# Rotating 96 images by 180 degrees: the first 2 KB of each row of the first load go through ACT's DMA queue

## The chip, the cores and the metric

The kernel runs on one core of a Trainium2 chip. The metric is device time in microseconds (us) of one execution. Before the change the median of three runs is 121.97 us (121.9 to 122.13).

## What is computed

```python
x = np.random.randn(32, 3, 256, 256).astype(np.float32)
out = np.rot90(x, k=2, axes=(-2, -1))
```

Each of the 96 images (256 x 256 float32, 256 KB) is turned by 180 degrees. Seen as one row of 65,536 numbers, an image is simply reversed. 25.17 MB are read and 25.17 MB are written; there is no arithmetic.

## The kernel before

An image is cut into four segments of E = 16,384 numbers (64 KB). A segment becomes a row of one SBUF partition, so 128 segments make a tile of 8.39 MB and three tiles hold everything: `A` and `Bt` hold the even and the odd segments of the first 64 images, `Ct` all segments of the last 32. Reversing an image means two things: the order of its four segments is reversed, which the stores do by their addresses (`::-1` in L53 to L54), and each segment is reversed within its row, which VectorE does in place.

Each tile is loaded by one DMA of 128 rows of 64 KB. Two DMA queues are in use. SyncE (SP) issues the loads of `A` (L64) and then `Ct` (L67), and after them every store; in the profile its queue is q1. ScalarE (ACT) issues only the load of `Bt` (L66); its queue is q10. Both queues feed the same 16 DMA engines, and each engine has 8 of the 128 rows of a tile. Within a queue the rows go in the order of their issue. Ahead of the load of `Bt` stands a VectorE memset of `Bt[:, 0:256]` (L65). The load overwrites what it wrote, so ACT has to wait for the memset before it issues.

`swap(t, lo, w)` (L56) exchanges the `w` numbers from `lo` on with their mirror image at the other end of the row, in three VectorE copies (L47): the far end reversed into the scratch tile `T`, the near end reversed into the far end, and `T` into the near end. `turn(t, lo, hi)` (L69) runs swaps of up to J = 2,048 numbers until `lo` reaches `hi`; half a row (8,192) makes a whole turn. The copies are kept in the order of the program (L47), which is written out by hand:

```python
turn(A, 0, half - J)        # L76: three of A's four swaps
store(A, 0, 0, LEAD)        # L77: 1 KB of each row, wants only the first swap
turn(Bt, 0, MID)            # L78: waits for the load of Bt
turn(A, half - J, half)     # L79: A's last swap
store(A, 0, LEAD, E)        # L80: the other 63 KB of each row
turn(Bt, MID, half)         # L81
store(Bt, 1, 0, E)          # L82
turn(Ct, 0, half)           # L83
store(Ct, 2, 0, E)          # L84
```

So the large store of `A` (L80) stands behind the first two swaps of `Bt` (L78) in VectorE's order, and all stores stand behind the load of `Ct` in SP's queue.

Of the kernel before, what the change touches and what calls it, by code (L numbers as in the profile page):

```python
# [2 lines left out]

os.environ.setdefault("NEURON_RT_ULTRASERVER_MODE", "4")

# [4 lines left out]


@with_exitstack
def kernel(
    ctx: ExitStack,
    tc: tile.TileContext,
    x: bass.AP,
    out: bass.AP,
):
    nc = tc.nc  # L20
    P = 128

    B, C, H, W = x.shape
    L = H * W
    G = 32
    E = L // 4
    J = E // 8

    xr = x.rearrange("b c h w -> (b c) (h w)").rearrange(
        "m (s e) -> (m s) e", s=4)  # L30
    om = out.rearrange("b c h w -> (b c) (h w)").rearrange(
        "m (s e) -> m s e", s=4)
    rows = 2 * P
    x4 = [xr[0:rows:2], xr[1:rows:2], xr[rows:rows + P]]
    o4 = [om[0:2 * G, 1::2], om[0:2 * G, 0::2], om[2 * G:3 * G]]

    pool = ctx.enter_context(tc.tile_pool(name="slots", bufs=1))
    A = pool.tile([P, E], x.dtype, tag="A")
    Bt = pool.tile([P, E], x.dtype, tag="B")
    Ct = pool.tile([P, E], x.dtype, tag="C")  # L40
    T = pool.tile([P, J], x.dtype, tag="T")

    def back(t, lo, hi):
        return t[:, hi - 1:(lo - 1 if lo else None):-1]

    def copy(dst, src):
        tc.keep_in_program_order(nc.vector.tensor_copy(out=dst, in_=src))  # L47

    def load(t, g, lo, hi, queue=nc.sync):
        return queue.dma_start(out=t[:, lo:hi], in_=x4[g][:, lo:hi])  # L50

    def store(t, g, lo, hi):
        return nc.sync.dma_start(  # L53
            out=o4[g][:, ::-1, lo:hi], in_=t[:, lo:hi])  # L54

    def swap(t, lo, w):  # L56
        hi = E - lo - w
        copy(T[:, 0:w], back(t, hi, hi + w))
        copy(t[:, hi:hi + w], back(t, lo, lo + w))
        copy(t[:, lo:lo + w], T[:, 0:w])  # L60

    MID = 2560
    LEAD = 256
    load(A, 0, 0, E)  # L64
    nc.vector.memset(Bt[:, 0:256], 0.0)  # L65
    load(Bt, 1, 0, E, nc.scalar)  # L66
    load(Ct, 2, 0, E)  # L67

    def turn(t, lo, hi):  # L69
        while lo < hi:  # L70
            w = min(J, hi - lo)
            swap(t, lo, w)
            lo += w

    half = E // 2
    turn(A, 0, half - J)  # L76
    store(A, 0, 0, LEAD)  # L77
    turn(Bt, 0, MID)  # L78
    turn(A, half - J, half)  # L79
    store(A, 0, LEAD, E)  # L80
# [6 lines that stand above are left out]
# [1 line left out]
_INS = ['x']  # L88
_OUTS = [((32, 3, 256, 256), 'float32')]


# [23 lines left out]
```

## Time and profile before

| what | value |
|---|---|
| device time, median of 3 runs | 121.97 us (121.9 to 122.13) |
| device time of the profiled execution | 121.9 us |
| its span | 120.1 us |
| VectorE busy | 44.9 us, 40 instructions |
| one 128x2048 copy | 1.23 us |
| DMA traffic | 50.33 MB, 1008 packets, mean 419 GB/s |
| load of `A`, from issue to landing | 38.7 us |
| load of `Bt` | 43.1 us |
| load of `Ct` | 60.1 us |

The span is what the profile shows from the first instruction to the last, and 1.8 us of the device time lie around it. In the profile's DMA lines a packet is one row of a transfer on one engine, or the 4-byte write with which an engine tells that its share of a transfer has landed; each transfer has 128 rows and 16 such writes, and seven transfers give 1008 packets. A DMA view of a stretch counts the packets that start in it, by queue. "SPq" and "ACTq" are the instructions with which SP and ACT issue transfers.

### The profile page before, as it was taken

To read this page: it belongs to the slowest core of one execution; us is meant where nothing else is said; L and a number is where in the kernel's file an instruction comes from. 1 tells how busy PE (TensorE), PEld (TensorE's weight loads), DVE (VectorE), ACT (ScalarE), POOL (GpSimd) and SP (SyncE) were. 2 spreads that over 40 slices of the span, in tenths; PEclk is the share of its full clock that TensorE was granted. 3 is DMA by queue.
4 is the path that set the end of the run, shared out by engine and by line. 5 is a ranking of instruction groups with operands and counts; after the bars stand their busy time and mean duration, and the time that the engine had idled before them with its cause. 6 is when DMAs were issued, how large, how long until landed. Compare 5 with 4: busy or idle time off the path is not lost.

```text
span 120.1 us, 97 instructions
## 1 busy us (share of the span) xinstructions
DVE 44.9 (37%) x40; POOL 0.2 (0%) x4
## 2 busy tenths in 40 slices
DVE  0000000000000899999999999999400000000000
POOL 0000000000000000000000000000000000000000
DMA  9888988898889988998899777988898889888980
GB/s 349 349 349 371 677 349 349 349 698 349 349 349 633 415 349 349 546 502 349 349 387 687 344 344 344 687 349 349 349 698 349 349 349 698 349 349 349 677 371 0
DMA packets 1008, 50.33 MB, mean 419 GB/s; under 512 B 112, under 2 KB 240, under 8 KB 240
## 3 DMA queue, kind: packets, MB, share of 16 engines
q1 hardware_dynamic: 864, 41.94, 81.3%
q10 hardware_dynamic: 144, 8.39, 16.1%
HBM read 25.17 MB, written 25.17 MB: 419 GB/s over the span
## 4 chain that ended last, share of the span: by engine, by line
DVE 38%; DMA 32%; issue 1%
DMA A<-in_x_dram 32%; DVE T L47 13%; DVE Bt L47 9%; DVE A L47 8%; DVE Ct L47 8%
## 5 line engine op out<-in xcount | busy, mean ns | idle before, releaser
L47 DVE COPY T<-A 128x2048 f32<-128x2048 f32 x4 | 4.9, 1226 | 38.4 <-DMA A<-in_x_dram 38.3
L47 DVE COPY T<-Bt 128x2048 f32<-128x2048 f32 (+2 forms) x5 | 5.1, 1014 | 0.2
L47 DVE COPY Bt<-T 128x2048 f32<-128x2048 f32 (+2 forms) x5 | 5.1, 1014 | 0.2
L47 DVE COPY Bt<-Bt 128x2048 f32<-128x2048 f32 (+2 forms) x5 | 5.1, 1013 | 0.2
L47 DVE COPY T<-Ct 128x2048 f32<-128x2048 f32 x4 | 4.9, 1227 | 0.1
L47 DVE COPY Ct<-T 128x2048 f32<-128x2048 f32 x4 | 4.9, 1227 | 0.1
L47 DVE COPY A<-T 128x2048 f32<-128x2048 f32 x4 | 4.9, 1227 | 0.1
L47 DVE COPY A<-A 128x2048 f32<-128x2048 f32 x4 | 4.9, 1227 | 0.1
L47 DVE COPY Ct<-Ct 128x2048 f32<-128x2048 f32 x4 | 4.9, 1226 | 0.1
L65 DVE MEMSET Bt<- 128x256 f32 x1 | 0.3, 272 | 0.9 <-PEq L99 0.9
L99 POOL MEMSET const-bfloat16-1.0<- 128x1 bf16 x1 | 0.1, 102 | 0.0
L99 POOL MEMSET const-uint8-127<- 128x1 uint8 x1 | 0.1, 102 | 0.0
L99 POOL MEMSET const-float32-0.0<- 128x1 f32 x1 | 0.1, 99 | 0.2 <-issue 0.2
L99 POOL MEMSET const-float32-1.0<- 128x1 f32 x1 | 0.1, 99 | 0.0
## 6 DMA issues: line engine op xcount, KB each, us to landing
out_dram<-A SPq DMA_DIRECT2D x1, 8064.0 KB, 20.9
out_dram<-A SPq DMA_DIRECT2D x1, 128.0 KB, 18.4
A<-in_x_dram SPq DMA_DIRECT2D x1, 38.7
Bt<-in_x_dram ACTq DMA_DIRECT2D x1, 43.1
Ct<-in_x_dram SPq DMA_DIRECT2D x1, 60.1
out_dram<-Bt SPq DMA_DIRECT2D x1, 29.6
out_dram<-Ct SPq DMA_DIRECT2D x1, 33.9
```

Source lines behind the costliest of these rows:

```text
L47: tc.keep_in_program_order(nc.vector.tensor_copy(out=dst, in_=src))
L65: nc.vector.memset(Bt[:, 0:256], 0.0)
L99: nc = _bacc.Bacc("TRN2", target_bir_lowering=False, num_devices=1)
```

## The change

The load of `A` is split by columns. SP loads columns 512 to 16,384 (62 KB of each row), and ACT loads columns 0 to 512 (2 KB of each row) ahead of its load of `Bt`. The memset is removed, so ACT's issues wait for nothing.

```diff
     MID = 2560
     LEAD = 256
-    load(A, 0, 0, E)
-    nc.vector.memset(Bt[:, 0:256], 0.0)
+    FIRST = 512
+    load(A, 0, FIRST, E)
+    load(A, 0, 0, FIRST, nc.scalar)
     load(Bt, 1, 0, E, nc.scalar)
     load(Ct, 2, 0, E)
```

In the program that is built, ACT issues two transfers in place of one, and neither waits for a semaphore. SP's order is as before. VectorE has one instruction less; its first copy (`T` from the far end of `A`) waits for the 62 KB transfer, and its second copy, which reads the near end of `A`, waits for the 2 KB transfer. The order of the copies and of the stores is the same. There are eight transfers in place of seven.

## The prediction

> **What bounds the kernel now.** I read the page first, then the DMA issues, then the DMA queues in short stretches of time, then the timeline of SP and VectorE.
>
> ```profile
> span 120.1 us, 97 instructions
> ...
> DMA  9888988898889988998899777988898889888980
> ...
> q1 hardware_dynamic: 864, 41.94, 81.3%
> q10 hardware_dynamic: 144, 8.39, 16.1%
> ```
>
> The two queues' packets fill 97.4% of the 16 DMA engines' time: the transfers are the bound, and there is no gap anywhere in the span. From q10, which carried only `Bt`, comes the price of a row: 16.1% of 120.1 us on 16 engines over 128 rows is 0.161 x 120.1 x 16 / 128 = **2.42 us for a 64 KB row** on its engine. An engine has 8 rows of each of 3 loads and 3 stores, 48 x 2.42 = 116 us. The page's chain of waits, which puts 38% on VectorE's copies, is misleading as a price list: those copies (44.9 us in all) lie beside transfers. They only matter where they keep the engines without a row to move.
>
> ```profile
> out_dram<-A SPq DMA_DIRECT2D x1, 8064.0 KB, 20.9
> out_dram<-A SPq DMA_DIRECT2D x1, 128.0 KB, 18.4
> A<-in_x_dram SPq DMA_DIRECT2D x1, 38.7
> Bt<-in_x_dram ACTq DMA_DIRECT2D x1, 43.1
> Ct<-in_x_dram SPq DMA_DIRECT2D x1, 60.1
> ```
>
> `A` and `Bt` land at nearly the same time (0.73 + 38.7 = 39.4 us, 1.16 + 43.1 = 44.3), `Ct` at 1.16 + 60.1 = 61.3. So the two queues share the engines while both have rows. How they share decides this case. Below are the DMA views of four stretches; each line is a queue with the packets that start in the stretch, their MB, and their share of it. First 4.5 to 5.5 us, then 7 to 7.8, then 9.5 to 10.2, then 38.4 to 40.6.
>
> ```profile
> q1 hardware_dynamic: 16, 1.05, 241.8%
> ```
>
> ```profile
> q10 hardware_dynamic: 16, 1.05, 302.4%
> ```
>
> ```profile
> q1 hardware_dynamic: 16, 1.05, 345.6%
> ```
>
> ```profile
> q10 hardware_dynamic: 16, 1.05, 109.9%
> q1 hardware_dynamic: 16, 0.00, 0.4%
> ```
>
> All 16 engines move one row of q1, then one of q10, then one of q1: the queues take turns, and **a turn is one row**. The last stretch shows more: q1's turn there is the 4-byte completion write of `A` (16 packets, 0.00 MB), and after these 4 bytes it is q10's turn again with the last row of `Bt`. A turn is counted in packets and not in bytes. The order on each engine is thus A A B A B A B A B A B A B A B, completion of `A`, B, C C C ...; the stretch from 1.5 to 3 us has one row of q1 on each engine, 4.5 to 5.5 the second, and q10 comes in third because ACT issues 0.43 us after SP.
>
> What feeds the engines when the loads are done? The rest of `A`, and only just:
>
> ```profile
> 59.76 0.55 SPq L53 DMA_DIRECT2D out_dram<-A  x1
> ```
>
> SP issues it at 59.76 us, when VectorE is done with `A`'s last swap, and the engines run out of loads and of the 128 KB lead store at 60.97 to 61.2 us, when the first 63 KB rows start. An issue takes about 1 us to become a first row (0.73 to 1.74 for `A`'s load), so there is next to no slack: whatever delays this issue leaves the engines empty.
>
> **The change part by part.** *Memset removed.* It costs 0.27 us on an idle VectorE, whose first copy starts at 39.47 us. Worth nothing itself. What it did is hold ACT's issue:
>
> ```profile
> 0.73 0.38 SPq L50 DMA_DIRECT2D A<-in_x_dram  x1
> 0.85 0.27 DVE L65 MEMSET Bt<- 128x256 f32 x1 [0.85 <-PEq L99]
> 1.16 0.38 ACTq L50 DMA_DIRECT2D Bt<-in_x_dram  x1
> 1.16 0.43 SPq L50 DMA_DIRECT2D Ct<-in_x_dram  x1
> ```
>
> Without it ACT issues the 2 KB rows at about 0.73, and `Bt` 0.43 later at 1.16, as now. SP's issue, with which the rows start at 1.74, is unmoved.
>
> *Rows.* The bytes are the same. SP's eight rows of an engine shrink from 64 to 62 KB, 8 x 2.42 x 2/64 = 0.60 us less. ACT's eight rows of 2 KB are not in the trace. The nearest are the lead store's 1 KB rows: eight of them and a completion write take the 0.65 us from 60.32 (first completion of `Ct`) to 60.97, 0.08 us each. At the large rows' rate 2 KB take 0.076; as the 1 KB row plus 1 KB more at that rate, 0.12. Eight cost 0.60 to 0.96 us, so the net is 0 to +0.36. Below nothing: the first row of `A` is followed by the second after 2.98 us (1.74 to 4.72), 0.57 more than a row, and small rows could fill that, so down to -0.57. I take +0.15, the middle of the first two ends. The added completion write (9 ns-sized in the 0.4% above) is nothing.
>
> *Turns.* This is the whole change. ACT's queue now begins with eight 2 KB rows. If each takes a turn, as the 4-byte write did, the order is A a A a ... (a is 2 KB), then C B C B ...: `A` no longer shares with `Bt`. `A` would land after 8 large rows in place of 15, 7 x 2.42 less the 0.15 = 16.8 us earlier, and VectorE would start at 39.47 - 16.8 = 22.7 us; its second copy up to one row later, if SP is a row ahead as now. `Bt` loses as much: it shares with `Ct` and comes last of the 24 large rows. Now the last of these is `Ct`'s, landing at 61.3; so `Bt` lands there, plus 0.15, plus 0.08 for a lead row that has its turn before `Bt`'s completion: 61.5 in place of 44.3.
>
> *What is behind that.* VectorE starts `A` at 22.7 and ends its three swaps near 34. Then it stands before `Bt`'s first swap (L78) until 61.5. Behind that wait in its order are `A`'s last swap and, through it, SP's issue of `A`'s 63 KB store; the only other thing in q1 is the lead store, 0.65 us of work. From `Bt`'s first copy to that issue the trace has 50.82 to 59.76 = 8.94 us (6 copies of 1.23, 3 of 0.43, 0.03 between them; hidden today under `Ct`'s rows). So the issue comes at 61.5 + 8.94 = 70.4. The first row follows an issue by 1.01 us for `A`'s load (0.73 to 1.74); an issue of a store takes 0.55 us where that took 0.38, so 1.0 to 1.2: first rows at 71.4 to 71.6, where they now are at 60.97. That is +10.5 to +10.7. An empty start may cost again what the first one did, 0 to 0.57: I take +0.3. Sum 10.6 + 0.3 = **+10.9 us**. Its ends: without the 0.15 and without a restart cost +10.3, with 0.36 for the small rows and the whole 0.57 +11.5; a start filled by small rows would take 0.57 off the low end, to +9.8.
>
> *Later.* `A`'s store then runs 8 x 2.38 = 19 us to about 91. `Bt`'s store is issued 10.55 us after `A`'s (70.31 - 59.76), at 81, `Ct`'s at 70.4 + 25.7 = 96.1 with `Bt`'s rows running to 110: no second gap. VectorE's early start on `A` buys nothing, as nothing of `A` but 128 KB may leave before L80.
>
> Against the profiled execution's 121.9 us (0.07 below the median of 121.97): 121.9 + 10.9 = **132.8 us**, bounds of this case 131.7 to 133.4.
>
> **The rivals.** *(1) The 2 KB rows go together (not slower).* If an engine takes ACT's small rows in one turn, or they are there before SP's first row and run ahead, only 0.6 to 0.96 us pass before `Bt` gets its turns against `A`. Then the order is A A a..a A B A B ...: `A` lands a row earlier and `Bt` a row later than now, 46.7, still before VectorE wants it at about 48.4 (37.05 + 11.35 of copies). The issue of `A`'s store stays ahead of 60.97. Time: 121.9 with -0.57 to +0.36, so 121.3 to 122.3. The point from which it decides is how many small rows pass without a large row of `A` between them: each brings `Bt` forward by 2.42 us, and from five of the eight on the gap of 10.9 is closed. For it: the trace has never had rows this small against another queue. Against it: the 4-byte write, smaller still, used up a turn, and no two rows of q10 ran together while q1 had any; SP's and ACT's issues come at the same time, and all 16 engines would have to do it, as VectorE waits for all.
> [...]
>
> *(2) A few small rows run ahead.* If one, two or three of the eight are through on every engine before SP's first row, `Bt` starts its turns so many rows earlier: 132.8 less 2.42 each, 130.4, 128.0 or 125.5 (four would leave 123.1). For it: without the memset ACT's issue is no longer later than SP's, and a small row takes a thirtieth of a large one. Against it: now SP had two rows in before q10's first, and SP issues no later.
>
> **How the numbers follow.** The forecast with its full gap has 0.76, rival 2 0.11 (0.08 of it for one or two rows), rival 1 0.13. The predicted time is the forecast's, 132.8. The range has to hold 8 in 10: the forecast's 131.7 to 133.4, 0.5 more above because the trace has no store that starts on empty engines (the 0.2 that I added for its issue could be some 0.7), and down to rival 2's two rows, less 0.2: 127.8 to 133.9. That holds the forecast but for its tails (0.72) and 0.08 of rival 2; rival 1 and three rows are left out. A measurement here tells about 0.2% (0.24 us) from no change. Rival 1's span of 121.3 to 122.3 splits into faster 0.03, same 0.08, slower 0.02; all else is slower: faster 0.03, same 0.08, slower 0.89.
>
> **What would show it.** Right: `A` lands near 22 to 25 us (the 2 KB part last), `Bt` near 61.5 together with `Ct`; VectorE's largest waits are two, some 22 us for `A` and some 26 for `Bt`; the issue of `A`'s 63 KB store is near 70.4; the DMA digits have about three slices near 0 from 61 to 71 us, and the queue's shares still sum to about 117 us of a span near 131; every later row is shifted by the gap. Wrong: `Bt` lands near 45 to 52, `A` near 37, and the digits stay full; or q10's first rows run together in the first 3 us. A gap of another length with `Bt` at 61.5 would mean that the price of the copies or of the restart is off.

## The result and the profile after

The changed kernel takes **132.75 us** (132.57 to 132.78, 5 runs) against 121.98 (121.9 to 122.34, 5 runs) beside it: ratio 1.0875, 95% interval 1.0864 to 1.0887. The profiled execution took 132.57 us with a span of 130.8, so the span grew by 10.7 us and what lies around it did not. The forecast was 132.8.

The page of the changed kernel: span, busy tenths of VectorE and DMA in 40 slices of 3.3 us, GB/s, and the two queues.

```profile
span 130.8 us, 99 instructions
...
DVE  0000001999300000002999999999930000000000
...
DMA  9799799797797797891007779779799797797790
GB/s 311 321 442 521 321 524 448 321 641 321 321 641 321 321 641 321 361 601 40 0 0 316 316 316 631 316 316 636 321 561 401 321 641 321 321 641 321 321 641 0
...
q1 hardware_dynamic: 864, 41.68, 74.3%
q10 hardware_dynamic: 288, 8.65, 15.3%
```

The hole is in the middle, at the 20th to the 22nd slice (62 to 72 us): engines that were never empty there now are. The queues together fill 89.6% of 130.8 us, 117.2 us, as before (97.4% of 120.1, 117.0). No work was added; time without work was. VectorE has a hole of its own just ahead of it.

The DMA issues of the changed kernel (engine, KB, us from issue to landing):

```profile
A<-in_x_dram SPq DMA_DIRECT2D x1, 7936.0 KB, 21.8
A<-in_x_dram ACTq DMA_DIRECT2D x1, 256.0 KB, 22.0
...
Bt<-in_x_dram ACTq DMA_DIRECT2D x1, 60.2
Ct<-in_x_dram SPq DMA_DIRECT2D x1, 60.0
```

`A` lands 17 us earlier than before (38.7) and `Bt` 17 us later (43.1), now together with `Ct`. The DMA view from 4.7 to 5.3 us (queue: packets started, MB, share) shows how:

```profile
q1 hardware_dynamic: 16, 1.02, 390.3%
q10 hardware_dynamic: 16, 0.03, 14.0%
```

Within this 0.6 us each engine starts one 2 KB row of q10 and one 62 KB row of q1. It goes on like that to the end of `A`: from 4 to 21.2 us each queue starts 112 rows, 7.11 MB and 0.23 MB. From 24 to 24.7 us `Bt` has its first row:

```profile
q10 hardware_dynamic: 16, 1.05, 345.4%
```

Before, that was at 7.14 us. What it costs is in the timeline of the changed kernel (start, us, instruction, idle time before it and what ended it), in SP's timeline from 66 to 72 us, and in the DMA views from 61.3 to 71 us and from 71 to 73:

```profile
22.53 1.23 DVE L47 COPY T<-A 128x2048 f32<-128x2048 f32 x1 [22.53 <-DMA A<-in_x_dram]
...
61.46 1.23 DVE L47 COPY T<-Bt 128x2048 f32<-128x2048 f32 x1 [27.62 <-DMA Bt<-in_x_dram]
...
66.63 1.23 DVE L47 COPY T<-A 128x2048 f32<-128x2048 f32 x1
...
70.41 1.23 DVE L47 COPY T<-Bt 128x2048 f32<-128x2048 f32 x1
```

```profile
70.40 0.54 SPq L53 DMA_DIRECT2D out_dram<-A  x1
```

```profile
DMA packets 0, 0.00 MB, mean 0 GB/s; under 512 B 0, under 2 KB 0, under 8 KB 0
```

```profile
q1 hardware_dynamic: 16, 1.03, 121.0%
```

VectorE waits 27.6 us for `Bt`, then does two swaps of `Bt`, then `A`'s last swap from 66.63 to 70.4. Only then can SP issue `A`'s 63 KB store, and from 61.3 to 71 us no row starts. The store's first rows start at 71.60 in place of 60.97, and each takes 1.21 x 2 = 2.42 us from the start.

### The profile page after: what moved, and what is told of

Same layout as the page of the kernel before. It is cut to its first block, busy times and chain, and to the rows that moved or that the text cites. A ratio compares the mean times of both kernels' runs of the same rounds, so it can differ in the third digit from the quotient of the medians.

```text
span 130.8 us, 99 instructions
## 1 busy us (share of the span) xinstructions
DVE 44.6 (34%) x39; POOL 0.2 (0%) x4
## 3 DMA queue, kind: packets, MB, share of 16 engines
q1 hardware_dynamic: 864, 41.68, 74.3%
q10 hardware_dynamic: 288, 8.65, 15.3%
## 4 chain that ended last, share of the span: by engine, by line
DVE 34%; another core or an unknown queue 21%; DMA 17%; issue 1%; DVEq 0%
DMA A<-in_x_dram 17%; DVE T L47 11%; DVE Bt L47 8%; DVE Ct L47 8%; DVE A L47 8%; DVEq L47 0%
## 5 line engine op out<-in xcount | busy, mean ns | idle before, releaser
L47 DVE COPY T<-Bt 128x2048 f32<-128x2048 f32 (+2 forms) x5 | 5.1, 1014 | 27.8 <-DMA Bt<-in_x_dram 27.6
L47 DVE COPY T<-A 128x2048 f32<-128x2048 f32 x4 | 4.9, 1227 | 22.6 <-DMA A<-in_x_dram 22.5
```

## Experiments

The theory: q1 and q10 take turns on every engine row by row whatever the rows' size, so eight small rows at the head of ACT's queue put `Bt` eight turns back (seven against before, where `A` was a row ahead already), and the loss is the gap before `A`'s store, which stands behind `Bt`'s first swaps. Times of before beside the experiments were 121.98 to 122.02 us.

### The memset alone removed

```diff
-    nc.vector.memset(Bt[:, 0:256], 0.0)
```

> Only the memset is removed; A is loaded whole by SP. Theory (queues take turns packet by packet, and what counts is which rows have their turns first): both issues come at 0.73 us, so the order is A B A B from the start, the second row of A is no longer ahead, A's completion write comes after Bt's eighth row, one turn of 2.42 us later than before. A lands near 41.9 us in place of 39.4, Bt too near 41.9 in place of 44.3; A's large store is issued at 62.2 in place of 59.76 and the engines are empty for about 2.3 us: 124.2 us (123.9 to 124.6). Rival (the loss of the change comes from the missing memset, not from the small rows): near 132.7. Rival (the memset is of no account): 121.9.

Measured **124.35 us** (124.26 to 124.64), ratio 1.0197 (1.0182 to 1.0212). The timeline of this kernel:

```profile
41.88 1.23 DVE L47 COPY T<-A 128x2048 f32<-128x2048 f32 x1 [41.88 <-DMA A<-in_x_dram]
```

and its DMA view from 4.5 to 5.5 us:

```profile
q10 hardware_dynamic: 16, 1.05, 241.9%
```

The second row of every engine is `Bt`'s, where it was `A`'s before. That one turn makes VectorE 2.41 us later (41.88 against 39.47) and the kernel 2.4 us slower. The memset was no dead weight: its 0.43 us of delay bought `A` a turn.

### The change with the memset put back

```diff
     load(A, 0, 0, FIRST, nc.scalar)
+    nc.vector.memset(Bt[:, 0:256], 0.0)
     load(Bt, 1, 0, E, nc.scalar)
```

> The changed kernel with the memset put back ahead of Bt's load. Theory: Bt's issue comes at 1.16 us with or without it, since ACT first issues the 2 KB rows, and all that decides is the eight small rows: 132.7 us (132.5 to 132.9), Bt landing near 61.4. Rival (the missing memset makes the loss): 121.9.

Measured **132.8 us** (132.62 to 132.83), ratio 1.0882 (1.0864 to 1.09). VectorE waits 27.6 us for `Bt`, as in the changed kernel. So the loss of the change is that of the small rows.

### The small rows on SP's queue

```diff
-    load(A, 0, FIRST, E)
-    load(A, 0, 0, FIRST, nc.scalar)
+    load(A, 0, 0, FIRST)
+    load(A, 0, FIRST, E)
     load(Bt, 1, 0, E, nc.scalar)
```

> The same split, but SP issues the 2 KB rows too, ahead of its 62 KB rows, and ACT issues only Bt, without a memset. Theory: now SP's queue spends eight turns on small rows while Bt moves a 64 KB row in each of its own, so the two change places: Bt lands near 22.5 us and A near 41.9, after 16 large rows. VectorE waits for A; its large store is issued near 62.2 and the gap is about 2.4 us: 124.3 us (123.9 to 124.8). Rival (the split into small rows costs in itself, whichever queue has them): near 132. Rival (SP's queue goes first whatever its rows are): A near 23 and 132 as well.

Measured **124.56 us** (124.48 to 124.85), ratio 1.0214 (1.0199 to 1.023). The issues of this kernel:

```profile
A<-in_x_dram SPq DMA_DIRECT2D x1, 7936.0 KB, 40.9
...
Bt<-in_x_dram ACTq DMA_DIRECT2D x1, 27.3
```

The two tiles have changed places, as a matter of which queue holds the small rows. The size for `Bt` was missed: 28 us in place of 22.5. From 1.5 to 3 us the trace has

```profile
q10 hardware_dynamic: 15, 0.98, 165.6%
q1 hardware_dynamic: 48, 0.10, 48.5%
```

Several engines had thus started two or more of SP's small rows before `Bt`'s first row, three on average; those rows went without a row of `Bt` between them, so that SP came to its large rows earlier and `Bt` shared its last turns with `A`. That is the mechanism of the prediction's second rival, seen here and not in the changed kernel.

### Unneeded rows in place of the split: eight, four, two

`A` is loaded whole again; ACT first loads 256 KB of the input into `T`, which nobody reads. The shape is 128 x 2 KB, 64 x 4 KB or 32 x 8 KB:

```diff
-    nc.vector.memset(Bt[:, 0:256], 0.0)
+    nc.scalar.dma_start(out=T[0:128, 0:512], in_=x4[2][0:128, 0:512])
```

> Before without the memset, A whole on SP, and ACT first loads 256 KB that nobody needs into T (128 rows of 2 KB, eight on each engine), then Bt. The extra 256 KB cost 0.6 us of the engines' time wherever they go. Theory: whose data the small rows carry is of no account, only that there are eight: as the changed kernel plus 0.6, A near 23, Bt near 62.0, A's large store issued near 71.0: 133.2 us (132.8 to 133.6). Rival (it is the split of A, its second copy's wait, or its shorter rows): near 122.5.

> As the kernel with eight unneeded rows, but the 256 KB are 64 rows of 4 KB, four on each engine. Theory (turns are counted in rows): Bt's completion comes after 21 large rows in place of 24, at about 54.8 us, A near 30; A's large store is issued near 63.7, the gap is about 3.3 us: 125.9 us (125.3 to 126.5). Rival (what counts is the bytes ahead of Bt): 133.2 as with eight rows.

> As above with 32 rows of 8 KB, two on each engine. Theory: Bt's completion after 19 large rows, near 49.9 us, A near 35; A's large store is issued near 58.9, ahead of the end of the loads: no gap, 122.5 us (122.3 to 122.8), before plus the 0.6 of the extra bytes. Rival (bytes): 133.2.

The load of `Bt` in the three kernels, in this order:

```profile
Bt<-in_x_dram ACTq DMA_DIRECT2D x1, 61.2
```

```profile
Bt<-in_x_dram ACTq DMA_DIRECT2D x1, 57.1
```

```profile
Bt<-in_x_dram ACTq DMA_DIRECT2D x1, 49.9
```

| rows on each engine | expected us | measured us |
|---|---|---|
| eight of 2 KB | 133.2 | 133.39 (133.34 to 133.51), ratio 1.0926 (1.0906 to 1.0945) |
| four of 4 KB | 125.9 | 127.08, 129.6, 129.81, 129.94 |
| two of 8 KB | 122.5 | 123.80 (123.74 to 123.8), ratio 1.014 (1.0125 to 1.0155) |

The same 256 KB cost 11.4, 5 to 8 and 1.8 us: it is the count of rows that counts, and neither the bytes, nor the split of `A`, nor its second copy's wait. The sizes of the two lower doses were missed, and the four runs with four rows fall apart into one of 127.08 and three near 129.8, so no ratio is given for them. In the profiled four-row run (129.6) `A` had two rows in before q10's first, as in before: from 4.5 to 6.5 us all 16 starts are q1's.

```profile
q1 hardware_dynamic: 16, 1.05, 120.9%
```

That is one turn more against `Bt`, 2.42 us. The six large rows that q1 starts on each engine from 4 to 21.2 us, four of them beside small ones, also took 15.7 us (91.3% of the stretch), 2.62 each in place of 2.42 and 1.2 us more in all. Together they make 129.5. The run of 127.08 is what one turn less would give, but it has no profile, so that is argued and not shown. With two rows the rows' times leave nothing for a gap between loads and stores, the loads just end later: from 4 to 21.2 us the four large rows of q1 on each engine took 10.9 us (63.6% of the stretch for 65 rows), 1.1 us more than at 2.42 each, and the two 8 KB rows themselves some 0.38 each (32.6% for q10, 5.61 us, less two rows of `Bt` at 2.42), which is about the 1.8 us lost. Beside the eight rows of 2 KB a large row took its 2.42 us (201.5% of the 1.2 us from 4.5 to 5.7). Fewer rows are here also longer rows, and rows on fewer partitions; which of the two makes the large rows slower was not tried.

### Half of `A`'s rows in transfers of their own

```diff
-    load(A, 0, FIRST, E)
-    load(A, 0, 0, FIRST, nc.scalar)
+    nc.sync.dma_start(out=A[0:64, 1024:E], in_=x4[0][0:64, 1024:E])
+    nc.sync.dma_start(out=A[64:P, 0:E], in_=x4[0][64:P, 0:E])
+    nc.scalar.dma_start(out=A[0:64, 0:1024], in_=x4[0][0:64, 0:1024])
```

> The changed kernel, but ACT loads the first 4 KB of only 64 of A's rows: the same 256 KB ahead of Bt, in four rows on each engine in place of eight. Theory (turns are counted in rows): Bt starts its turns four rows earlier, lands 4 x 2.42 = 9.7 us earlier at about 51.8, A later at about 32; A's large store is issued at about 60.7 in place of 70.4 and the gap shrinks from 10.5 to about 1 us: 123.0 us (122.4 to 123.6). Rival (the share goes by bytes, or the 256 KB ahead of Bt cost the time): 132.7.

Measured **147.55 us** (146.97 to 151.08), ratio 1.2079 (1.2041 to 1.2118): neither theory. The DMA view from 4 to 34 us:

```profile
DMA packets 142, 8.12 MB, mean 271 GB/s; under 512 B 15, under 2 KB 15, under 8 KB 15
```

That is from the profiled execution, the one of 151.08 us. The two queues moved 271 GB/s where 419 was usual, and 251 from 34 to 64 us, as long as `A`'s 64-row transfers ran against `Bt`; from 68 to 85 us, with `Ct` alone, it was 432. ACT's small rows were nearly all through before SP's first rows besides (79 starts of q10 against 15 of q1 up to 4.2 us), so the dose was not what I meant it to be. Thus it tests nothing about turns; the dose was repeated with the unneeded rows. Why 64-row transfers of large rows are that slow was not tried.

### `A` finished and stored before `Bt` is waited for

The changed kernel's loads, another order behind them:

```diff
     store(A, 0, 0, LEAD)
-    turn(Bt, 0, MID)
     turn(A, half - J, half)
     store(A, 0, LEAD, E)
+    turn(Bt, 0, MID)
     turn(Bt, MID, half)
```

> The changed kernel with its loads untouched, but VectorE does A's last swap, and SP issues A's 63 KB store, ahead of Bt's first swaps. Theory (the loss lies wholly in that A's store stands behind the wait for Bt): Bt still lands at 61.4, but A's store is issued near 37.7 and its rows follow the lead rows at 61.0 without a gap; Bt's turn then ends at 76.6, before A's store has left at 80: 122.0 us (121.8 to 122.2). Rival (the turns or the small rows cost in themselves): near 132.7. Rival (part of the loss is elsewhere): between.

Measured **122.83 us** (122.71 to 123.22), ratio 1.0074 (1.006 to 1.0088). `Bt` lands as late as in the changed kernel (VectorE starts it at 62.60), yet 9.9 of 10.8 us are back. The loss lay in what stood behind the wait. But 0.8 us are not back, and the next two kernels show the same.

### All loads on SP's queue, and `A` in one store

```diff
-    nc.vector.memset(Bt[:, 0:256], 0.0)
-    load(Bt, 1, 0, E, nc.scalar)
+    load(Bt, 1, 0, E)
```

> Before without the memset, and SP issues all three loads in the order A, Bt, Ct; ACT issues nothing. Theory: no turns, so A lands after its own 8 rows near 22.5 us and Bt after 16 near 41.5, both ahead of VectorE's need; A's large store is issued near 50 and the engines have no gap: 121.9 us (121.7 to 122.1), no gain over before since the engines were never empty there. Rival (two queues feed the engines better than one): some per cent slower.

Measured **122.97 us** (122.82 to 123.11), ratio 1.0079 (1.0066 to 1.0091). With, besides, `turn(A, 0, half)` and `store(A, 0, 0, E)` ahead of `Bt`'s turn:

> As the kernel with all loads on SP in order, and A turned whole and stored by one DMA of 64 KB rows, without the 1 KB lead store. Theory: A's turn ends near 37.7, long before the loads end at 60.3, so the lead store is not needed; its eight 1 KB rows of an engine cost 0.65 us for 0.30 us of data, and its going saves 0.35: 121.55 us (121.4 to 121.7), the fastest here. Rival (the lead rows cost nothing): 121.9.

Measured **122.98 us** (122.89 to 123.29), ratio 1.0083 (1.0069 to 1.0096). They missed by 1.1 and 1.4 us. In all three kernels the last load row of each engine is long. Its DMA view is that from 57.5 to 59 us, in which each engine starts this one row; the share times 1.5 us is its mean time. First before, then `A` first, one queue, one queue with one store of `A`:

```profile
q1 hardware_dynamic: 16, 1.05, 161.6%
```

```profile
q10 hardware_dynamic: 16, 1.05, 220.9%
```

```profile
q1 hardware_dynamic: 16, 1.05, 242.3%
```

```profile
q1 hardware_dynamic: 16, 1.05, 241.3%
```

2.42 us before, and 3.31, 3.63 and 3.62 in the three. In these, large store rows had been issued at 38 to 51 us and waited for the loads to end; in before they are issued at 59.76 and are there when the loads have ended. Standing behind a load in the same queue is not enough: with `A` first, q1's rows, among them those of `Ct` ahead of the store in SP's queue, took no longer in all than in the changed kernel (80.0% of 121.2 us, 97.0, against 74.3% of 130.8, 97.2), and only q10 took longer (17.3%, 21.0 us, against 15.3%, 20.0), by about what its row, the engine's last load row, has over 2.42 us.

### The store of `A` issued late

One queue as above, with one number changed so that `A`'s last swap ends later:

```diff
-    MID = 2560
+    MID = 7168
```

> The kernel with all loads on SP, with MID at 7168 in place of 2560, so that A's large store is issued near 59.5 us in place of 51. That kernel and the two others whose A store was issued long before the loads' end (at 37 to 51) took 1.0 us more than forecast, and in them the last load row of each engine took 3.1 to 3.9 us in place of 2.42. Theory (large store rows that already stand in the queue behind the last load row cost about 1 us at the change from loads to stores, and a store that comes just as the loads end doesn't): 121.9 us (121.7 to 122.1), last load row 2.42. Rival (the 1 us comes of the single queue, or of stores issued early in general): 122.9 to 123.0.

Measured **122.0 us** (121.72 to 122.24, 12 runs), ratio 0.9996 (0.9986 to 1.0007). `A`'s store is issued at 59.3, and the last load row, in the same view:

```profile
q1 hardware_dynamic: 16, 1.05, 175.7%
```

takes 2.64 us, 0.2 more than in before; where these come from was not shown. The 1 us thus comes with large store rows that wait while the last load rows go, and not with the single queue. What happens within an engine then, the traces do not show.

Last, the same without the lead store:

```diff
-    store(A, 0, 0, LEAD)
     turn(Bt, 0, MID)
     turn(A, half - J, half)
-    store(A, 0, LEAD, E)
+    store(A, 0, 0, E)
```

> The kernel with all loads on SP and the late store of A, without the 1 KB lead store: A leaves in one store of 64 KB rows, issued near 59.3 us. Theory: the lead rows' 0.37 us of an engine (eight of 0.046) go, and the store's first rows can be there at 59.3 + 1.19 = 60.5, while the last load rows end at 60.6 to 61.05; a part of the cost of a waiting store row comes back. 121.8 us (121.5 to 122.0), at best 0.3% under before. Rival (any large store row that waits behind the last load row costs the whole 1 us): 122.6 to 122.9.

Measured **122.08 us** (121.98 to 122.3, 11 runs), ratio 1.0007 (0.9998 to 1.0016). The last load row is back at 2.42 us (161.6% in the same view), but the lead rows' 0.37 us did not come off: `A`'s store is issued at 59.23 us in place of 59.76, and the profiled span is 120.2 us against 120.1. Little was there to be had: the 1 KB of each row goes in the large row now, and in before a store row of 64 KB takes 2.42 us (242.3% of the 1 us from 115.9 to 116.9) where one of 63 KB takes 2.38 (79.4% of the 9 us from 71 to 80 for three), 0.3 us for eight. The same 0.3 us is left out of the forecast for one queue with one store of `A`. No version beat the kernel before.

## Why the prediction was right

- **Turns of one row.** Right within 0.2 us: VectorE's first copies of `A` and `Bt` were forecast at 22.7 and 61.5 us and came at 22.53 and 61.46. `Bt` landed 17.1 us later than before, seven rows of 2.42, and its completion writes are in by 61.0 us, 19.5 later than without the memset (by 41.5), eight rows. The unneeded rows show it without the split.
- **SP a row ahead.** Left open in the prediction. Without the memset SP was not ahead: q10's first row came second, so the 2 KB part did not hold up the second copy (23.79, right behind the first).
- **Small rows' price.** +0.15 us was taken, and it is about +0.06: from 4.7 to 5.3 us a 2 KB row took 0.084 us (14.0% of 0.6) and a 62 KB row 2.342 (390.3%), 0.008 more than a 64 KB row, eight times. The first completion of `Ct` moved by 0.05 (60.32 to 60.36). The price of a lead row was read wrong on the way: in the changed kernel q1's eight lead rows and two completion writes take 0.39 us of an engine (12.9% of the 3 us from 59 to 62), 0.046 a row and not 0.08. In before, the rest of the 0.65 us was the wait for `A`'s large store, whose first row comes 1.21 us after its issue there (59.76 to 60.97).
- **The chain behind `Bt`.** 8.94 us of copies were forecast, and 61.46 to 70.40 is that. Issue to first row was put at 1.0 to 1.2, and is 1.20 (70.40 to 71.60).
- **Restart.** The mis-sized term. I added 0.3 us because the very first rows of the kernel are slow (2.98 us from the first to the second in before). The store's first rows took 2.42 us, where its later ones took 2.39: next to nothing. The first 63 KB rows moved by 71.60 - 60.97 = 10.63, the span by 10.7, against a forecast of 10.9. The upper end of issue to first row made up for part of it, and 132.8 is nearer to the measured 132.75 than that because it was counted from the profiled 121.9, not from the 121.98 beside it.
- **Later.** `Bt`'s and `Ct`'s stores were forecast at 81 and 96.1 us and issued at 80.95 and 96.09; no second gap.
- **Memset.** "Worth nothing itself" holds for its 0.27 us. But the wait that it made was worth 2.4 us to the kernel before; the change lost that too, and it does not show, since the small rows decide the turns alone (132.8 with the memset put back).
- **Rivals.** The small rows neither went together nor ran ahead. On all 16 engines together q1 and q10 started 112 and 112 rows from 4 to 21.2 us beside the small rows of 2 KB (and as many beside the unneeded ones), 96 and 81 beside those of 4 KB, 65 and 80 beside those of 8 KB, the last two with 16 completion writes of q10 counted in: one for one to within one an engine. Running ahead was seen with the small rows on SP's queue, where 48 of them had started by 3 us beside 15 rows of `Bt`.

## What to carry to other kernels

Where two DMA queues are busy at once, as here, count rows and not bytes: here ACT's queue gave eight turns away to rows of 2 KB, 0.084 us each, and `Bt` behind them came eight rows of 2.42 us later than without them. Then look at which instruction waits for the late tile and what is queued behind it; moving `A`'s store ahead of that wait brought 9.9 of the 10.8 us back with the same late load. And before an idle-looking instruction is removed, ask what its wait was ordering: the 0.27 us memset held a turn of 2.4 us.

## What the runs showed of the hardware beside that

Large store rows that already wait when an engine does its last load row went with a row 0.9 to 1.2 us longer (3.31 to 3.63 us against 2.42); with a store issued at 59.2 to 59.8 us, as the loads ended, it took 2.42 to 2.64. Where transfers of 64 rows of 60 to 64 KB ran against a 128-row load, the queues moved 271 GB/s (4 to 34 us) and 251 (34 to 64) in the execution that was profiled, in place of before's mean of 419. And `A`'s store, which starts on empty engines in the changed kernel, has its first rows 1.20 us after its issue (1.21 in before, where the engines had just been busy), and these take 2.42 us where its later ones take 2.39, while the first load of before has 2.98 us from its first row to its second.
